# Keeping the transposed x in DRAM and moving 1/rms behind the input projections

## The chip, the cores and the metric

The kernel runs on one core of a Trainium2 chip. The metric is the time of one launch in microseconds on the device; the times before are a median of three runs. Engines are named as in the profile: PE (TensorE matmuls), PEld (its weight loads), DVE (VectorE), ACT (ScalarE), POOL (GpSimd) and SP (the engine whose queue issues most transfers).

## The reference

One layer of a decoder on 1024 prompt tokens and 64 sample tokens (8 sequences of 8), with D = 1024:

```
h     = x * rsqrt(mean(x*x) + eps) * g_mix            # RMS norm, per token
proj  = h @ w_in                                      # 1024 -> 1024 (RWKV) + 768 (conv) + 1536 (attention)
RWKV:      xs = p + (prev_token(p) - p) * mu_shift, then the recurrence on r, k, v, decay, a, g
short conv: u = c * x ; y = sum_j conv_w[j] * u[t-2+j] ; out = b * y
attention:  q = rmsnorm(q), k = rmsnorm(k) per head of 64; stick-breaking weights over k, v
x = x + concat(outputs) @ w_out
x = x + relu(rmsnorm(x) @ w_up)^2 @ w_down
x = x + sigmoid(rmsnorm(x) @ w_ple_gate) * (p @ w_ple_proj)
```

All is float32. Outputs are the new x for prompt and sample, the new key and value rows, and the recurrent states.

## The kernel before, in words

Activations stand transposed in SBUF, features on the partitions and tokens along a row. Each float32 operand of a large matrix product is split into a rounded part (`hi`) and its remainder (`lo`), and each product takes three matmuls: hi with hi, hi with lo, lo with hi.

The stages, in program order:

- **Front (L181 to L202).** Nine tiles of 128 tokens (the last has 64). Each is loaded (`x_tile`, four buffers `xt`), squared and summed on ACT (L189), and 1/rms is taken (L190, L192). DVE multiplies x by 1/rms and by the gain, which stands in `gbc` on all partitions (L193). PE transposes the result in eight 128x128 blocks (L198), ACT rounds it into `hT[0]` (L200), and DVE writes the remainder to `hT[1]` (L201).
- **RWKV projections (`rw_tile`, L319).** Eight tiles of 128 columns, each in three token chunks (`CH`: 384, 384, 320). A chunk is 24 matmuls (`gemm_t`, L169 to L171) into one of three PSUM banks (`acc`). ACT then reads the bank twice: a copy to `raw` (L330) and a product with 1 - mu to `xs` (L333, scale `om`); DVE adds mu times the shifted row (L334). `om` comes from the parameter rows, which PE transposes at L218. The first two tiles (`dwa`, `dg`) use the weights `w_da`. The weight loader `W.load` takes one transfer into `wr` (two buffers), a rounding on ACT (L158) and a subtraction on POOL (L159).
- **Recurrence and attention projections (`project`, L786 on).** The recurrent chain alternates with 30 projections whose results have tokens on the partitions: two tiles of 128 tokens by 256 columns to a bank (two banks, `gemm_sb`). ACT copies the bank to `nat` (L802), and for q and k it also squares it (L805).
- **Convolution and first attention half (`convolution`, L975 on, and `attention`).** The two generators take turns. For c the bank is copied to `cc` by ACT (L987); for x DVE multiplies the bank by `cc` into `ue` (L1002); for b DVE multiplies the bank by the convolved result `y` (L1027), which goes to `mix_s` in DRAM. In the attention, POOL sets masks (L920), DVE scans (L922), PE transposes the weights (L942).
- **MLP.** `Part` A holds tokens 0 to 511, `Part` B the other 576. `load_x` (L1292) reads x a second time from the input, in pieces of 128 tokens by 512 features (`xr`, four buffers shared with other temporaries), transposes each in four blocks on PE (L1302) and copies it to `self.x` on ACT (L1303). `load_mix` reads `mix_s` (L1287) and splits it; `out_proj` adds its products onto `self.x` (L1395). Part A's `load_x` stands at the end of the first attention half, part B's after the decoding attention.

The instructions of each engine run in a fixed order. A planner makes that order from the program and a model of durations: it issues what is ready by its own clock, in program order of priority, and takes the buffers as they become free. A wait on one instruction therefore holds everything behind it on the same engine or queue.

Of the kernel before, what the change touches and what calls it, by code (L numbers as in the profile page):

```python
# [48 lines left out]
def hybrid_step(ctx: ExitStack, tc: tile.TileContext, I, O):  # L49
# [6 lines left out]
    def f(t):  # L56
        return t.bitcast(F32)
# [38 lines left out]
    mix_s = dram.tile([8, 128, T], F32, name="mix_s")  # L96

# [8 lines left out]

    def x_tile(i):
        r = 128 if i < 8 else NS
        xt = xpool.tile([128, D], F32, name="xt", bufs=4)
# [4 lines left out]
    gbc = xpool.tile([128, D], F32, name="gbc")  # L114
    gm = I["g_mix"]
    SP.dma_start(gbc, bass.AP(tensor=gm.tensor, offset=gm.offset, ap=[[0, 128], [1, D]]))
# [59 lines left out]
    def w_cols(c0):  # L176
        return W.load(w_in[:, c0:c0 + 256])
# [3 lines left out]
    for i in range(9):  # L181
        if i == 1:
            w_da = w_cols(768)
        if i + 3 < 9:
            xts.append(x_tile(i + 3))
        xt, r = xts[i]
        st = xpool.tile([128, 2], F32, name="st", bufs=5)
        h = xpool.tile([128, D], F32, name="h", bufs=3)
        S.activation(h[:r], xt[:r], AF.Square, accum_out=st[:r, 0:1])  # L189
        S.activation(st[:r, 1:2], st[:r, 0:1], AF.Sqrt, bias=eps_rms[:r], scale=1.0 / D)  # L190
        rs = xpool.tile([128, 1], F32, name="rs", bufs=5)
        V.reciprocal(rs[:r], st[:r, 1:2])  # L192
        V.scalar_tensor_tensor(h[:r], xt[:r], rs[:r], gbc[:r], op0=ALU.mult, op1=ALU.mult)  # L193
        for g in range(2):
            pt = tr().rearrange("p (k t) -> p k t", k=4)
            for k in range(4):
                c = (4 * g + k) * 128
                PE.transpose(pt[:, k, :r], h[:r, c:c + 128], ident[:r, :r])  # L198
            dst = slice(i * 128, i * 128 + r)
            S.copy(hT[0][g][:, :, dst], pt[:, :, :r])  # L200
            V.tensor_sub(hT[1][g][:, :, dst], pt[:, :, :r], f(hT[0][g][:, :, dst]))  # L201
# [117 lines left out]
    def rw_tile(w, m, ct):  # L319

        raw = pe_tile("raw")
        xs = pe_tile("xs")
        G.memset(raw[:, 0:1], 0.0)
        rs3 = raw[:, E1:E1 + NB * 9].rearrange("p (b j) -> p b j", j=9)
        G.tensor_copy(rs3[:, :, 0], shT[:, ct, :])
        for t0, n in CH:
            ps = acc()
            gemm_t(ps, w, m, hT, t0, n)
            np_ = min(n, NP - t0)
            S.copy(raw[:, 1 + t0:1 + t0 + np_], ps[:, :np_])  # L330
            if np_ < n:
                S.copy(rs3[:, :, 1:9], ps[:, np_:n].rearrange("p (b j) -> p b j", j=NJ))
            S.activation(xs[:, t0:t0 + n], ps[:, :n], AF.Copy, scale=om[:, ct:ct + 1])  # L333
# [452 lines left out]
    def project(hf, n, w, i0):  # L786
# [15 lines left out]
        S.copy(flat, ps)  # L802
        if n < 2:
            sq = sbp.tile([128, 512], F32, name="sq", bufs=1)
            S.square(sq[:, :256 * ni], ps)  # L805
# [169 lines left out]
    def convolution():  # L975
# [3 lines left out]
        cc, ue, yu = [], [], []  # L979
        w = W.load(w_in[:, CV0 + 256:CV0 + 512])  # L980
        for j in range(2):
            t = cv.tile([128, LW], F32, name="cc", bufs=2)
            cc.append(t)
            for t0, n in CH:
                ps = gemm_cv()
                gemm_t(ps, w, j, hT, t0, n)
                S.copy(t[:, t0:t0 + n], ps[:, :n])  # L987
                yield
        w = W.load(w_in[:, CV0 + 512:CV0 + 768])
        for j in range(2):  # L990
            u = cv.tile([128, LW], F32, name="ue", bufs=2)
            ue.append(u)
# [28 lines left out]
        for j in range(2):  # L1021
            y = cc[j]
            for t0, n in CH:
# [239 lines left out]
    class Part:  # L1263
# [28 lines left out]
        def load_x(self, bank):  # L1292
            t0 = self.t0
            for i in self.tiles:
                r = 128 if i < 8 else NS
                for g in range(2):
                    xt = self.tmp("xr")
                    c = slice(g * 512, g * 512 + 512)
                    SP.dma_start(xt[:r], xp_in[i * 128:i * 128 + 128, c] if i < 8 else xs_in[:, c])
                    pt = bank().rearrange("p (k t) -> p k t", k=4)  # L1300
                    for k in range(4):
                        PE.transpose(pt[:, k, :r], xt[:r, k * 128:k * 128 + 128], ident[:r, :r])  # L1302
                    S.copy(self.x[:, 4 * g:4 * g + 4, i * 128 - t0:i * 128 - t0 + r], pt[:, :, :r])  # L1303
# [181 lines left out]
    A.load_x(acc)  # L1485
# [21 lines left out]
    B.load_x(tr)  # L1507
# [117 lines left out]
```

## Time and profile before

| | us |
|---|---|
| median of 3 runs | 1701.94 |
| lowest, highest | 1698.44, 1704.59 |
| profiled execution: span from first to last instruction | 1705.2 |
| profiled execution: own time | none is listed beside the span |
| PE busy | 1642.1 |
| DVE busy | 1055.6 |
| ACT busy | 790.8 |
| POOL busy | 698.7 |
| mean granted TensorE clock | 0.989 |

Shares are averages over stages with different limits, so the stages have to be read apart. The front ends at about 40 us, the RWKV projections run to about 160, recurrence and attention projections to about 440, convolution and first attention half to about 585, then come the second half, the decoding attention, the MLP and the gate. In the lines shown further down, a row of the timeline gives the start and length in us, the engine, the line and the operands, and in brackets how long the engine had been idle and for whom. A row of a group gives the total busy time and the mean length in ns. A row of waits gives the total in us, the number of waits and the longest. PE's records of matmuls are pipelined: the distance between starts, not the length of one, is what a matmul costs.

### The profile page before, as it was taken

What the parts mean: (1) busy time and instruction counts of PE and PEld (TensorE: products, weight loads), DVE (VectorE), ACT (ScalarE), POOL (GpSimd) and SP (SyncE); (2) the same over time, 40 slices, a digit from 0 to 9 for tenths busy, and PEclk for the clock granted to TensorE, in tenths of its full rate; (3) what the DMA queues carried; (4) which work ended last, traced back from release to release, by engine and by line L of the source; (5) the groups of instructions that cost most, each with busy time, mean ns of one, the idle gap of its engine ahead of it and who ended that gap; (6) DMA issues with size and microseconds to landing.
All of it is one profiled execution on the core that took longest, in us unless ns stands there. A gap on an engine that the chain in (4) does not pass through costs nothing.

```text
span 1705.2 us, 30695 instructions
## 1 busy us (share of the span) xinstructions
PE 1642.1 (96%) x11901; PEld 1481.8 (87%) x11901; DVE 1055.6 (62%) x1830; ACT 790.8 (46%) x1563; POOL 698.7 (41%) x754
## 2 busy tenths in 40 slices
PE   6999899999899898999999999999999999999998
PEld 5899888889888777888886777988999999999898
DVE  6266844555277749888853435277777777767432
ACT  6633433343354657666643344464543434437421
POOL 4123121123232565443334563356755455538210
PEclk9999999999999999999999999999999999999999
DMA  5144466325513764344235565422322322222211
GB/s 189 37 132 115 142 166 184 73 79 147 167 56 101 222 181 125 117 130 126 78 103 158 173 187 172 130 84 78 100 88 86 94 92 87 88 84 90 72 45 41
DMA packets 207060, 197.03 MB, mean 116 GB/s; under 512 B 58113, under 2 KB 172449, under 8 KB 206786
## 3 DMA queue, kind: packets, MB, share of 16 engines
q1 hardware_dynamic: 197186, 174.08, 34.4%
q0 software_dynamic: 5120, 16.78, 3.3%
q10 hardware_dynamic: 4608, 4.20, 1.0%
q8 instruction: 94, 1.54, 0.4%
q14 instruction: 52, 0.43, 0.1%
HBM read 158.03 MB, written 36.98 MB: 114 GB/s over the span
## 4 chain that ended last, share of the span: by engine, by line
PE 77%; DVE 9%; DMA 5%; ACT 3%; issue 3%; POOL 2%; SPq 2%; ACTq 0%; DVEq 0%; POOLq 0%
PE b L1093 13%; PE b L1095 13%; PE b L1094 12%; PE b L1440 3%; PE b L1442 3%; PE b L1441 3%; PE b L169 3%; PE b L170 3%; PE b L171 3%; PE b L797 2%; PE b L795 2%; PE b L796 2%; PE b L942 2%; DMA wr<-in_w_in 1%; DVE keep L922 1%
## 5 line engine op out<-in xcount | busy, mean ns | idle before, releaser
L1074 POOL TENSOR_TENSOR wl<-wr,wh 128x512 fp32r<-128x512 f32 x172 | 241.2, 1412 | 266.5 <-ACT wh L1073 227.7
L1073 ACT CAST wh<-wr 128x512 fp32r<-128x512 f32 x292 | 178.3, 621 | 300.6 <-PE b L1094 194.3
L1093 PE MATMUL b<-ah,wh 128*128 128x288 f32 (+1 forms) x768 | 253.6, 331 | 4.8 <-DVE x L1480 3.8
L1480 DVE TENSOR_TENSOR x<-b,x 128x288 f32<-128x288 f32 (+1 forms) x384 | 198.8, 528 | 90.9 <-PE b L1095 88.2
L1095 PE MATMUL b<-ah,wl 128*128 128x288 f32 (+1 forms) x768 | 252.3, 329 | 0.0
L1094 PE MATMUL b<-al,wh 128*128 128x288 f32 (+1 forms) x768 | 251.9, 328 | 0.0
L1093 PE MATMUL b<-nh,wh 128*128 128x512 f32 (+1 forms) x448 | 165.8, 370 | 3.1 <-DVE x L1480 1.4
L1094 PE MATMUL b<-nl,wh 128*128 128x512 f32 (+1 forms) x448 | 165.1, 369 | 0.0
L1095 PE MATMUL b<-nh,wl 128*128 128x512 f32 (+1 forms) x448 | 164.6, 368 | 0.0
L1093 PEld LDWEIGHTS b<-ah,wh 128*128 128x128 f32 x768 | 144.4, 188 | 17.3 <-DVE x L1480 6.6
L1095 PEld LDWEIGHTS b<-ah,wl 128*128 128x128 f32 x768 | 144.4, 188 | 10.1
L1094 PEld LDWEIGHTS b<-al,wh 128*128 128x128 f32 x768 | 144.5, 188 | 9.5 <-DVE al L1408 0.3
L795 PE MATMUL b<-wh,h_hi 128*128 128x256 f32 x432 | 127.6, 295 | 5.3 <-ACT sq L805 5.3
L797 PE MATMUL b<-wh,h_lo 128*128 128x256 f32 x432 | 126.9, 294 | 0.0
L796 PE MATMUL b<-wl,h_hi 128*128 128x256 f32 x432 | 124.8, 289 | 0.0
L169 PE MATMUL b<-h_hi,wh 128*128 128x384 f32 (+1 forms) x336 | 115.4, 344 | 1.9 <-ACT xs L333 1.3
L159 POOL TENSOR_TENSOR wl<-wr,wh 128x1024 fp32r<-128x1024 f32 x26 | 64.8, 2508 | 124.1 <-ACT wh L158 124.1
L1074 DVE TENSOR_TENSOR wl<-wr,wh 128x512 fp32r<-128x512 f32 x120 | 97.8, 817 | 28.1 <-ACT wh L1073 27.2
L170 PE MATMUL b<-h_lo,wh 128*128 128x384 f32 (+1 forms) x336 | 114.3, 340 | 0.3 <-DVE h_lo L201 0.3
L171 PE MATMUL b<-h_hi,wl 128*128 128x384 f32 (+1 forms) x336 | 113.2, 337 | 0.0
L922 DVE TENSOR_TENSOR_SCAN keep<-keep,onesq 128x128 f32<-128x128 f32 (+3 forms) x64 | 95.6, 1494 | 21.4 <-POOL keep L920 20.9
L1093 PEld LDWEIGHTS b<-nh,wh 128*128 128x128 f32 x448 | 84.3, 188 | 18.6 <-DVE x L1480 2.5
(427 smaller groups left out, 4284.6 us busy)
## 6 DMA issues: line engine op xcount, KB each, us to landing
wr<-in_w_up SPq DMA_DIRECT2D x64, 512.0 KB
wr<-in_w_down SPq DMA_DIRECT2D x64, 512.0 KB
wr<-in_w_in SPq DMA_DIRECT2D x26, 512.0 KB
wr<-in_w_out SPq DMA_DIRECT2D x16, 512.0 KB
xt<-in_x_prompt SPq DMA_DIRECT2D x8, 512.0 KB
stk_s<-sth ACTq DMA_DIRECT2D x32, 128.0 KB
stk_s<-stl SPq DMA_DIRECT2D x32, 128.0 KB
v_s<-spl SPq DMA_DIRECT2D x16, 256.0 KB
```

The lines of the kernel that those rows point to most:

```text
L169: PE.matmul(ps[:, :n], wh[:, k, c], a, start=(k == 0), stop=False)
L170: PE.matmul(ps[:, :n], wh[:, k, c], b, start=False, stop=False)
L171: PE.matmul(ps[:, :n], wl[:, k, c], a, start=False, stop=(k == nk - 1))
L795: PE.matmul(o, a, w[0][:, k, :], start=(k == 0), stop=False)
L796: PE.matmul(o, a, w[1][:, k, :], start=False, stop=False)
L797: last = PE.matmul(o, b, w[0][:, k, :], start=False, stop=(k == 7))
L1073: S.copy(h3, src)
L1074: (sub or G).tensor_sub(l3, src, f(h3))
L1093: PE.matmul(ps[:, :n], w(0, k, m), a, start=(k == 0), stop=False)
L1094: PE.matmul(ps[:, :n], w(0, k, m), b, start=False, stop=False)
L1095: PE.matmul(ps[:, :n], w(1, k, m), a, start=False, stop=(k == nk - 1))
L1480: V.tensor_add(p.x[:, m, t0:t0 + n], ps[:, :n], p.x[:, m, t0:t0 + n])
```

## The change

Three things are done together.

1. **x is transposed once, raw.** In the front, PE transposes x as loaded. DVE and ACT evacuate one half each into `xT` (256 tokens, two buffers). Per block of 128 features, ACT makes `hi` = x times g (the gain is now a column `gmT`, a scale of the activation), DVE makes `lo`. `xT` is stored to a new DRAM tensor `x_s` by ACT's queue. The squares come after that, in place, and leave 1/rms in the columns of `rsc`. `xt` has three buffers in place of four, the 512 KB load of `gbc` becomes one of 4 KB.
2. **1/rms goes to the results.** Nine small matmuls spread `rsc` over the partitions as `rbc` (128 x 1088), which is also stored to DRAM (`rb_s`). `rw_tile`: DVE multiplies the bank by `rbc` into `raw`; ACT makes `xs` from `raw`. `project`: the copy and the square become one ACT operation for each 128 tokens, with the column of `rsc` as scale. `convolution`: c is multiplied by `rb` (read back from `rb_s`) on DVE and once more on POOL, so that c times x has both factors; the result of b is multiplied by `rb` on POOL.
3. **The residual is read from `x_s`.** `load_x` becomes four transfers for each part, without transposes and copies.

```
-    for i in range(9):
-        if i == 1:
-            w_da = w_cols(768)
...
-        S.activation(h[:r], xt[:r], AF.Square, accum_out=st[:r, 0:1])
-        S.activation(st[:r, 1:2], st[:r, 0:1], AF.Sqrt, bias=eps_rms[:r], scale=1.0 / D)
-        V.reciprocal(rs[:r], st[:r, 1:2])
-        V.scalar_tensor_tensor(h[:r], xt[:r], rs[:r], gbc[:r], op0=ALU.mult, op1=ALU.mult)
...
-            S.copy(hT[0][g][:, :, dst], pt[:, :, :r])
-            V.tensor_sub(hT[1][g][:, :, dst], pt[:, :, :r], f(hT[0][g][:, :, dst]))
+    def x_sums(i):
+        xt, r = xts[i]
+        st = xpool.tile([128, 2], F32, name="st", bufs=5)
+        S.activation(xt[:r], xt[:r], AF.Square, accum_out=st[:r, 0:1])
+        S.activation(st[:r, 1:2], st[:r, 0:1], AF.Sqrt, bias=eps_rms[:r], scale=1.0 / D)
+        V.reciprocal(rsc[:r, i:i + 1], st[:r, 1:2])
+    for i0 in range(0, 9, 2):
+        ids = range(i0, min(9, i0 + 2))
+        t0, n = 128 * i0, min(256, T - 128 * i0)
+        if i0 == 2:
+            w_da = w_cols(768)
+        xT = xpool.tile([128, 8, 256], F32, name="xT", bufs=2)
+        for i in ids:
+            if i + 3 < 9:
+                xts.append(x_tile(i + 3))
+            xt, r = xts[i]
+            for g in range(2):
+                pt = tr().rearrange("p (k t) -> p k t", k=4)
+                for k in range(4):
+                    c = (4 * g + k) * 128
+                    PE.transpose(pt[:, k, :r], xt[:r, c:c + 128], ident[:r, :r])
+                dst = xT[:, 4 * g:4 * g + 4, 128 * (i - i0):128 * (i - i0) + r]
+                if g:
+                    S.copy(dst, pt[:, :, :r])
+                else:
+                    V.tensor_copy(dst, pt[:, :, :r])
+        for k in range(8):
+            hi, lo = (h[k // 4][:, k % 4, t0:t0 + n] for h in hT)
+            S.activation(hi, xT[:, k, :n], AF.Copy, scale=gmT[:, k:k + 1])
+            V.scalar_tensor_tensor(lo, xT[:, k, :n], gmT[:, k:k + 1], f(hi), op0=ALU.mult, op1=ALU.subtract)
+        S.dma_start(x_s[:, :, t0:t0 + n].rearrange("k p t -> p k t"), xT[:, :, :n])
+        for i in ids:
+            x_sums(i)
+    for t0, n in CH:
+        pt = tr()
+        for t in range(t0, t0 + n, 128):
+            r = min(128, T - t)
+            PE.matmul(pt[:, t - t0:t - t0 + r], rsc[:r, t // 128:t // 128 + 1].to_broadcast([r, 128]), ident[:r, :r],
+                      start=True, stop=True)
+        S.copy(rbc[:, t0:t0 + n], pt[:, :n])
+    S.dma_start(rb_s, rbc)
...
@@ rw_tile
-            S.copy(raw[:, 1 + t0:1 + t0 + np_], ps[:, :np_])
+            V.tensor_mul(raw[:, 1 + t0:1 + t0 + np_], ps[:, :np_], rbc[:, t0:t0 + np_])
+            S.activation(xs[:, t0:t0 + np_], raw[:, 1 + t0:1 + t0 + np_], AF.Copy, scale=om[:, ct:ct + 1])
...
-            S.activation(xs[:, t0:t0 + n], ps[:, :n], AF.Copy, scale=om[:, ct:ct + 1])
@@ project
-        S.copy(flat, ps)
+        for i, sc in enumerate(scales):
+            S.activation(nat[:, i], ps[:, 256 * i:256 * i + 256], AF.Copy, scale=sc)
...
-            S.square(sq[:, :256 * ni], ps)
+            for i, sc in enumerate(scales):
+                S.activation(sq[:, 256 * i:256 * i + 256], ps[:, 256 * i:256 * i + 256], AF.Square, scale=sc)
@@ convolution
+        rb = cv.tile([128, T], F32, name="rb")
+        SP.dma_start(rb, rb_s)
...
-                S.copy(t[:, t0:t0 + n], ps[:, :n])
+                V.tensor_mul(t[:, t0:t0 + n], ps[:, :n], rb[:, t0:t0 + n])
+                G.tensor_mul(t[:, t0:t0 + n], t[:, t0:t0 + n], rb[:, t0:t0 + n])
...
                 V.tensor_mul(y[:, t0:t0 + np_], ps[:, :np_], y[:, t0:t0 + np_])
+                G.tensor_mul(y[:, t0:t0 + np_], y[:, t0:t0 + np_], rb[:, t0:t0 + np_])
...
@@ Part
-        def load_x(self, bank):
...
+        def load_x(self):
+            for m in range(0, 8, 2):
+                SP.dma_start(self.x[:, m:m + 2], x_s[m:m + 2, :, self.t0:self.t0 + self.n].rearrange("k p t -> p k t"))
```

More of the change, by code (lines that the diff above doesn't have):

```diff
@@ L96, in hybrid_step @@
     mix_s = dram.tile([8, 128, T], F32, name="mix_s")
+    x_s = dram.tile([8, 128, T], F32, name="x_s")
+    rb_s = dram.tile([128, T], F32, name="rb_s")
     xp_in = I["x_prompt"][0]
@@ L113, in hybrid_step @@
     xts = [x_tile(0)]
-    gbc = xpool.tile([128, D], F32, name="gbc")
+    grow = xpool.tile([8, 128], F32, name="grow")
     gm = I["g_mix"]
-    SP.dma_start(gbc, bass.AP(tensor=gm.tensor, offset=gm.offset, ap=[[0, 128], [1, D]]))
+    SP.dma_start(grow, bass.AP(tensor=gm.tensor, offset=gm.offset, ap=[[128, 8], [1, 128]]))
     xts += [x_tile(i) for i in range(1, 3)]
@@ L180, in hybrid_step @@
     S.activation(pcs[:, 0, 0:1], eps_rms, AF.Sqrt)
-    for i in range(9):
-        if i == 1:
-            w_da = w_cols(768)
-        if i + 3 < 9:
-            xts.append(x_tile(i + 3))
+    rsc = consts.tile([128, 10], F32)
+    rbc = rp.tile([128, T], F32, name="rb_all")
+    gmT = xpool.tile([128, 8], F32, name="gmT")
+    pt = tr()
+    PE.transpose(pt[:, :8], grow, ident[:8, :8])
+    S.copy(gmT, pt[:, :8])
+    def x_sums(i):
         xt, r = xts[i]
         st = xpool.tile([128, 2], F32, name="st", bufs=5)
-        h = xpool.tile([128, D], F32, name="h", bufs=3)
-        S.activation(h[:r], xt[:r], AF.Square, accum_out=st[:r, 0:1])
+        S.activation(xt[:r], xt[:r], AF.Square, accum_out=st[:r, 0:1])
@@ L190, in hybrid_step @@
         S.activation(st[:r, 1:2], st[:r, 0:1], AF.Sqrt, bias=eps_rms[:r], scale=1.0 / D)
-        rs = xpool.tile([128, 1], F32, name="rs", bufs=5)
-        V.reciprocal(rs[:r], st[:r, 1:2])
[L193 to L201, printed above, removed]
+        V.reciprocal(rsc[:r, i:i + 1], st[:r, 1:2])
@@ L202, in hybrid_step @@
+    for t0, n in CH:
+        pt = tr()
+        for t in range(t0, t0 + n, 128):
[4 more added lines that the diff above has]
+    S.dma_start(rb_s, rbc)
+    S.copy(rsc[64:128, 9:10], rsc[0:64, 8:9])
+    S.copy(rsc[0:64, 9:10], rsc[64:128, 7:8])
     xpool.release()
@@ L978, in convolution @@
         CV0 = 1024
-        cc, ue, yu = [], [], []
+        cc, ue = ([cv.tile([128, LW], F32, name=n_, bufs=2) for j in range(2)] for n_ in ("cc", "ue"))
+        rb = cv.tile([128, T], F32, name="rb")
+        SP.dma_start(rb, rb_s)
         w = W.load(w_in[:, CV0 + 256:CV0 + 512])
         for j in range(2):
-            t = cv.tile([128, LW], F32, name="cc", bufs=2)
-            cc.append(t)
+            t = cc[j]
             for t0, n in CH:
@@ L990, in convolution @@
         for j in range(2):
-            u = cv.tile([128, LW], F32, name="ue", bufs=2)
-            ue.append(u)
+            u = ue[j]
             us3 = u[:, NP + 2:LW].rearrange("p (b j) -> p b j", j=NJ + 2)
@@ L1031, in convolution @@
                                  y[:, NP + 2:NP + 2 + NB * 10].rearrange("p (b j) -> p b j", j=10)[:, :, 0:NJ])
+                    G.tensor_mul(ue[j][:, 0:NS], ue[j][:, 0:NS], rb[:, NP:T])
                 yield
@@ L1290, in load_mix @@
                 V.tensor_sub(lo, t, f(hi))
-        def load_x(self, bank):
[L1293 to L1303, printed above, removed]
+        def load_x(self):
+            for m in range(0, 8, 2):
+                SP.dma_start(self.x[:, m:m + 2], x_s[m:m + 2, :, self.t0:self.t0 + self.n].rearrange("k p t -> p k t"))
         def norm(self, gain, bank, wide=False, pool=False):
@@ L1484, in hybrid_step @@
     A = Part(xpa, wka, hpa, 0, 512, ((0, 512),))
-    A.load_x(acc)
+    A.load_x()
     A.load_mix(range(0, 4))
@@ L1506, in hybrid_step @@
     B.load_mix(range(8))
-    B.load_x(tr)
+    B.load_x()
     out_proj(A, 4, 4)
```

9 lines of the change are left out of this document (7 added, 2 removed).

## The prediction

> **What bounds the kernel now.** I read the head and first part of the page, then the windows by stage.
>
> ```profile
> span 1705.2 us, 30695 instructions
> PE 1642.1 (96%) x11901; PEld 1481.8 (87%) x11901; DVE 1055.6 (62%) x1830; ACT 790.8 (46%) x1563; POOL 698.7 (41%) x754
> ...
> 0.00:40.00 40.00, 24.77 (x130) 21.81 (x130) 26.30 (x39) 26.34 (x54) 20.01 (x47) 0.96 0.64 202
> 40.00:100.00 60.00, 59.16 (x333) 54.08 (x334) 20.08 (x32) 34.16 (x59) 9.81 (x12) 0.97 0.11 37
> 100.00:160.00 60.00, 59.60 (x488) 58.07 (x487) 42.17 (x51) 26.09 (x44) 21.95 (x18) 1.00 0.44 140
> 160.00:440.00 280.00, 270.48 (x2880) 248.40 (x2879) 155.89 (x356) 98.53 (x204) 59.75 (x59) 0.98 0.52 136
> 440.00:555.00 115.00, 109.86 (x837) 97.49 (x838) 67.84 (x125) 50.55 (x110) 35.81 (x78) 0.97 0.33 95
> 555.00:605.00 50.00, 43.51 (x266) 36.72 (x264) 32.66 (x87) 30.22 (x68) 31.73 (x45) 0.97 0.70 216
> 1060.00:1085.00 25.00, 24.54 (x178) 22.87 (x177) 12.07 (x16) 14.25 (x25) 8.05 (x6) 1.00 0.66 217
> ```
>
> Columns of the windows: busy time of PE, PEld, DVE, ACT, POOL, then granted clock, DMA share, GB/s. TensorE is the bound nearly everywhere. The largest single loss is the front: 40 - 24.8 = 15.2 us idle, a quarter of the 63.1 us that PE is idle in the whole span (1705.2 - 1642.1). So the change is worth what it takes off PE where PE is full (1060 to 1085), plus what it does to the order in the front; where PE already waits (555 to 605), less.
>
> **Part 1, the second reading of x.** load_x (L1292) goes for both parts: 72 transposes, 18 ACT copies, 18 loads. Four plain loads per part replace them.
>
> ```profile
> 1064.16 0.60 PE L1302 MATMUL b<-ident,xr 128*128 128x128 f32 x4
> 1064.52 0.38 PE L1093 MATMUL b<-mh,wh 128*128 128x288 f32 x1
> 1075.52 2.32 PE L1302 MATMUL b<-ident,xr 128*128 128x128 f32 x16 [0.42 <-DMA xr<-in_x_prompt]
> 1077.77 0.40 PE L1093 MATMUL b<-mh,wh 128*128 128x288 f32 x1
> 1081.16 0.46 PE L1302 MATMUL b<-ident,xr 64*128 64x64 f32 x4
> PE b L1302 <- DMA xr<-in_x_prompt: 4.0, 2, 3.0
> 576.58 0.73 PE L1093 MATMUL b<-mh,wh 128*128 128x512 f32 x1
> 575.03 5.42 POOL L1074 TENSOR_TENSOR wl<-wr,wh 128x512 fp32r<-128x512 f32 x3 [0.92 <-ACT wh L1073]
> ```
>
> Part B (1060 to 1085): a group of four costs PE 0.36 us (1064.16 to 1064.52). Five such groups make 1.8; the run of 16 takes 2.25 (1075.52 to 1077.77) after a wait of 0.42; the last four some 0.4. Together 4.8 us. PE is busy 24.54 of 25 us there, so all of it comes off the end; the loads stay hidden if the DMA, busy 0.66 of its time, still brings w_out in time. If that cover fails, the bound is 0.
>
> Part A (555 to 605): 32 transposes at 0.09 are 2.9 us, and PE also waits 4.0 us for xr, 6.9 at most. But PE is already idle 6.5 us in this window, and the first out_proj matmul at 576.58 follows the weight split that starts on POOL at 575.03, which no transpose delays. So most of it turns into another wait. I take 2, bounds 0 and 6.9. The x loads (4 times 512 KB) still stand on SP's queue ahead of the mix loads, about as many bytes as today's.
>
> **Part 2, the front.** Today a tile goes: square, sqrt, reciprocal, times gain, transpose, round (ACT), remainder (DVE).
>
> ```profile
> 19.24 0.67 PE L169 MATMUL b<-h_hi,wh 128*128 128x384 f32 x1
> 24.07 0.34 PE L171 MATMUL b<-h_hi,wl 128*128 128x384 f32 x1
> 30.26 0.44 PE L169 MATMUL b<-h_hi,wh 128*128 128x384 f32 x1 [0.63 <-ACT h_hi L200]
> 36.93 1.73 PE L198 MATMUL b<-ident,h 128*128 128x128 f32 x16
> 38.84 0.85 DVE L221 TENSOR_SCALAR om<-par 128x8 f32<-128x8 f32 x1
> 39.73 1.05 ACT L333 ACTIVATE xs<-b,om 128x384 f32<-128x384 f32 x2 [0.48 <-DVE h_lo L201]
> 40.37 0.45 PE L169 MATMUL b<-h_hi,wh 128*128 128x384 f32 x1 [0.39 <-ACT xs L333]
> L189 ACT ACTIVATE h<-xt x9: 1051/1059/1082, 4.7 to 30.6; 128x1024 f32<-128x1024 f32 x8, 64x1024 f32<-64x1024 f32 x1
> L200 ACT CAST h_hi<-b x18: 392/584/618, 9.2 to 38.8; 128x512 fp32r<-128x512 f32 x16, 128x256 fp32r<-128x256 f32 x2
> L1316 ACT ACTIVATE nh<-x,par 128x512 fp32r<-128x512 f32 x8 | 5.5, 731 | 0.0
> L1453 ACT ACTIVATE c<-c 128x288 f32<-128x288 f32 x64 | 27.9, 442 | 24.2 <-DVE c L1452 24.2
> L852 ACTq DMA_DIRECT2D stk_s<-sth x32: 582/620/877, 188.2 to 414.0; - x32
> ```
>
> A 24-matmul chunk takes 4.2 us at full rate (19.24 to 24.07 with a cold start is 4.8); 16 transposes take 1.73. Until 40.37 PE has done 72 transposes (7.8 us) and two chunks (8.4): 24 us of 40 are lost, idle or at half rate. One cause is in the last three timeline rows: the bank of the first chunk is read twice, by the copy (L330) and by xs (L333), which needs om; om comes only at 39, so the dg tile, next on that bank, starts at 40.37. In the new kernel one DVE product frees the bank; xs reads raw from SBUF.
>
> New cost on ACT for two tiles: eight roundings of 128x256, estimated at 0.45 each (0.442 for 128x288, 0.731 for 128x512), 3.6; two evacuations 1.2; two squares with their small operations 2.8; one store issue 0.6. That is 8.2 against some 5.2 today. Four pairs, a last tile of about 4, and 4 for weight casts: 41 us from 4.7 on, so ACT ends at 46 if never idle. The squares also release xt, now three slots: tile 4 can load only after the square of tile 1, and so on.
>
> But squares can fill ACT's gaps, and PE is no longer held to two chunks. Laying the operations out by these durations: first GEMM at about 18, dg's first chunk at 25 (after the 1/rms of tiles 0 to 2), second chunks from 28 to 38, last chunk at 37 to 44. By 44 PE would have done five full chunks (20.8), one of 320 columns (3.5) and the transposes: 32 us, 12 lost, so 12 better. That is one end. The other: strict program order with ACT at 46, 46 - 16 = 30 lost, 6 worse. I take 5 better, nearer the middle than the layout, because the order is fixed beforehand and loads that come late hold a whole queue. The nine broadcasts (nearest row, a 0.11 us transpose) and the gain's transpose fall into idle time: 0; without it 1 to 2. The 4.45 MB store of x_s on ACT's queue shares the DMA engines (0.64 busy now, near nothing from 40 to 100): its cost is in the bounds.
>
> **Part 3, scaling the results.** The eight RWKV tiles: 24 copies leave ACT, 24 products of about 0.55 go to DVE (13 us).
>
> ```profile
> L447 DVE TENSOR_TENSOR xs<-b,xs x6: 482/548/558, 122.8 to 174.2; 128x384 f32<-128x384 f32 x4, 128x320 f32<-128x320 f32 x2
> PE b L795 <- ACT sq L805: 5.3, 1, 5.3
> ACT sq L805 <- DVE xs L447: 11.6, 1, 11.6
> L802 ACT COPY nat<-b 128x512 f32<-128x512 f32 x24 | 14.0, 585 | 53.2 <-PE b L797 51.7 <-issue 1.4
> L802 ACT COPY nat<-b 128x256 f32<-128x256 f32 x6 | 2.2, 372 | 12.0 <-PE b L797 11.0 <-ACT ss L808 1.0
> DVE AB L515 <- PE b L512: 18.4, 1, 18.4
> L1454 POOL TENSOR_TENSOR al<-c,ah 128x288 fp32r<-128x288 f32 x64 | 57.0, 902 | 25.6 <-ACT ah L1454 25.6
> POOL beta L920 <- ACT beta L915: 39.4, 19, 8.4
> PE b L942 <- DVE beta L924: 3.5, 1, 3.5
> ```
>
> Three banks of 4.2 us each cover the longer read-out (DVE product, then ACT, then DVE). Without cover the pattern is the one in rows two and three: DVE late, ACT waits in order 11.6, PE stands 5.3. I take 1, bounds 0 and 5. In the projections two 256-wide passes cost ACT 0.74 against 0.585, about 0.16 more, 24 times for nat and 16 times for sq: 6.4 us, behind two banks of 5 us. ACT also moves the recurrent chain there, so 1, bounds 0 and 4. In the convolution cc moves to DVE, whose queue stands up to 18.4 us at L515; rb must land before the first product. Twelve POOL products of about 1.1 (0.902 for 288 columns) and two small ones, 13.5 us, stand between the masks (L920) of the attention; POOL waits 39.4 us for ACT there, which covers most. Behind a late mask wait DVE's scan and then PE, as in the last row. The last product also delays the mix store by 1.1, with SP's queue behind it. I take 2, bounds 0 and 6. A gain here is excluded: nothing leaves PE.
>
> A row and a rule at this place: one front product took 3.16 us, others 1.28, while POOL worked beside it.
>
> ```profile
> 14.34 3.16 DVE L193 SCALAR_TENSOR_TENSOR h<-xt,rs,gbc 128x1024 f32<-128x1024 f32 x1
> 14.06 5.67 POOL L159 TENSOR_TENSOR wl<-wr,wh 128x1024 fp32r<-128x1024 f32 x2 [4.27 <-ACT wh L158]
> ```
>
> If every one of the fourteen POOL products held DVE for its length, 13.5 us would be added on DVE between 440 and 555, beyond my bound of 6. The Trainium skill, page "SBUF — State Buffer", section "Who interferes with whom", states it: GpSimd and a VectorE operation with two SBUF inputs exclude each other for a whole instruction. By that rule, the trace agrees in this one row.
>
> **The sum**, on the profiled execution: -4.8 (B) -2 (A) -5 (front) +1 (RWKV) +1 (projections) +2 (convolution) = -7.8, so a span of 1697.4. That execution's span lies 3.3 us above the median of the three runs, 1701.94 (nothing else around it is listed). I forecast 1701.94 - 7.8 = 1694 for the median.
>
> **Rivals.** (a) No change: the front's gain is eaten by ACT, part A's by other waits. Then -4.8 (B) + 4 (part 3) = -1, 1701. For it: ACT's 41 us in a front of 40. Against it: the bank held until 40.37. (b) Slower through one mechanism: ACT becomes the front's bound. The loads wait for squares behind eight roundings, and PE keeps program order: +6, with part B and A still won (-6.8) and the full bound of part 3's costs that also sit on ACT and DVE (+9): about +8, 1710. It decides once the last group's roundings end after about 49 (44 of the layout plus the 5 taken). (c) POOL's products hold the attention's scans: +13.5 in place of +2, so +4, 1706. (d) The transposes of both parts only covered waits, so that removing them frees nothing: -7.8 + 6.8, again 1701.
>
> **Chances.** Forecast 0.5; (a) and (d) together 0.28; (b) 0.15; (c) 0.07. A change under 0.3% (5 us) can't be told from none by this measurement. The forecast's own range is 1683 to 1699; its upper end is within 0.3%, and the better end of the front is 7 us beyond its middle. The range that leaves out 2 in 10 reaches 1681 to 1709. Faster 0.51, same 0.29, slower 0.2.
>
> **What would show it.** Right: L1302's line gone, out_proj of part B without gaps; PE's idle time in 0:40 under 12 us; dg's matmuls before 35 us; 440 to 555 no more than 2 us longer. Wrong: ACT over 36 us busy in 0:40 with PE waiting for the roundings; xt loads issued later than 30 us; PE waiting for mixl or wr in place of xr; longer waits of L922 for L920. A reordering of the planner far from the edits would make all of it wrong, in either direction.

## The result and the profile after

The change made the kernel slower: 1709.16 us (median of 11 runs, 1705.03 to 1710.62) beside 1702.35 for the kernel before in the same session, a ratio of 1.0043 (95% interval 1.0028 to 1.0057), +6.8 us. A second timing on another chip gave 1.0066 (1.0045 to 1.0087). The forecast was 1694, so it was wrong in sign; the time is near rival (b)'s 1710.

The profiled execution of the changed kernel lists 1709.11 beside its span of 1707.4. If the kernel before also lies 1.7 us above its span, its profiled execution took 1706.9, more than each of its 11 timed runs there (1695.94 to 1706.36). So differences between the two traces understate the loss; sizes of a whole kernel are taken from the timings.

The head of the page and the windows of the changed kernel, in the prediction's stages and columns:

```profile
span 1707.4 us, 30670 instructions
PE 1641.2 (96%) x11848; PEld 1476.5 (86%) x11848; DVE 1067.6 (63%) x1890; ACT 793.8 (46%) x1592; POOL 708.4 (41%) x768
...
0.00:40.00 40.00, 23.51 (x125) 20.27 (x125) 17.84 (x38) 31.39 (x69) 16.42 (x45) 1.00 0.84 273
40.00:100.00 60.00, 57.97 (x328) 52.15 (x328) 26.85 (x59) 32.94 (x63) 6.44 (x8) 0.97 0.19 65
160.00:440.00 280.00, 269.94 (x2928) 247.42 (x2923) 153.16 (x349) 110.92 (x248) 63.89 (x58) 0.98 0.51 135
440.00:555.00 115.00, 109.01 (x791) 96.14 (x791) 67.85 (x131) 44.63 (x98) 45.01 (x84) 0.96 0.35 100
555.00:605.00 50.00, 43.29 (x257) 35.90 (x256) 38.83 (x96) 26.05 (x61) 26.59 (x49) 0.80 0.67 211
1060.00:1085.00 25.00, 22.15 (x138) 19.66 (x137) 13.18 (x18) 10.74 (x17) 9.13 (x7) 1.00 0.74 252
```

53 matmuls have left PE (11901 to 11848 instructions), but its busy time has hardly moved (1642.1 to 1641.2). In the front PE now has 16.5 idle us of 40 instead of 15.2. ACT's share of the first 40 us rose from 26.3 to 31.4, and split in two it shows where. The windows of the changed kernel, and the waits of its first 60 us:

```profile
0.00:20.00 20.00, 7.37 (x32) 6.28 (x33) 4.00 (x9) 11.99 (x24) 11.90 (x41) 1.00 0.75 245
20.00:40.00 20.00, 16.14 (x95) 13.99 (x93) 13.83 (x30) 19.40 (x45) 4.51 (x5) 1.00 0.93 300
```

```profile
PE b L213 <- DMA xt<-in_x_prompt: 15.2, 5, 7.3
```

```profile
SPq L114 <- ACT st L196: 5.1, 2, 3.1
```

ACT is busy 19.40 of 20 us between 20 and 40, but only 11.99 of the first 20. PE's transposes stand 15.2 us for tiles of x, 4.6 of them for the first tile; the last row, of SP's queue, shows loads of x (L114) that stand for ACT. The timeline says more, and what the first bank waits for:

```profile
7.43 1.06 ACT L195 ACTIVATE xt<-xt 128x1024 f32<-128x1024 f32 x1
11.90 0.23 SPq L247 DMA_DIRECT2D prow<-in_gn_b  x1
12.26 0.36 SPq L114 DMA_DIRECT2D xt<-in_x_prompt  x1
18.63 3.96 PE L213 MATMUL b<-ident,xt 128*128 128x128 f32 x16 [7.26 <-DMA xt<-in_x_prompt]
22.25 0.53 PE L173 MATMUL b<-h_hi,wh 128*128 128x384 f32 x1
27.77 0.33 SPq L114 DMA_DIRECT2D xt<-in_x_prompt  x1
32.02 1.11 SPq L114 DMA_DIRECT2D xt<-in_x_sample  x1
38.91 0.46 ACT L232 COPY rb_all<-b 128x384 f32<-128x384 f32 x1
40.61 0.43 DVE L218 COPY xT<-b 128x256 f32<-128x256 f32 x1 [3.22 <-PE b L213]
42.85 0.54 DVE L364 TENSOR_TENSOR raw<-b,rb_all 128x384 f32<-128x384 f32 x1
43.45 0.69 PE L173 MATMUL b<-h_hi,wh 128*128 128x384 f32 x1
50.06 0.41 PE L173 MATMUL b<-h_hi,wh 128*128 128x320 f32 x1
```

PE's longest wait for x, 7.26 us until 18.63, is for the fourth tile. Its load (12.26) does not wait for a square: the first tile's square (L195) runs at 7.43, ahead of all roundings. The load stands in SP's queue behind the small loads of the parameter rows (`prow`, the last at 11.90), which waited 6.1 us for earlier transfers; in the kernel before, with four buffers, this load stands ahead of those rows and goes out before 3.4. Three later loads (23.73, 27.77 and 32.02) do wait for squares, 6.3 us in all, each issued as a square ends. The first matmul of the projections (the GEMM below) comes at 22.25 (before: 19.24). The first bank, held for `om` before, is now held for the broadcast 1/rms until 39.37, and then by the fixed order of DVE, which stands 3.22 us for the last tile of x and has other work ahead of the product: product at 42.85, next group at 43.45 instead of 40.37. The last chunk starts at 50.06.

To see where time goes from there I use an **offset**: for each ACT and DVE instruction that both traces have, its start in the changed kernel less its start in the kernel before, and the median of these over a stretch. All are worked out against the one profiled execution of the kernel before. The last column gives the time of the profiled execution, and behind it the median of that kernel's runs.

| kernel | 100 to 130 | 130 to 160 | 540 to 560 | 650 to 700 | 880 to 930 | 1030 to 1060 | 1090 to 1200 | end | profiled, median |
|---|---|---|---|---|---|---|---|---|---|
| the changed kernel | 5.6 | 4.4 | 9.3 | 8.0 | 8.4 | 2.7 | 1.8 | 2.0 | 1709.11, 1709.16 |
| the same, other chip | 4.1 | 2.9 | 8.4 | 7.2 | 7.7 | 8.6 | 7.2 | 6.9 | 1713.97, 1717.39 |
| x_slots | 4.5 | 3.4 | 5.8 | 9.4 | 9.8 | 10.9 | 9.3 | 9.9 | 1716.99, 1710.13 |
| front_dve | 3.5 | 2.5 | 0.0 | 5.3 | 5.6 | 1.6 | 0.3 | 1.1 | 1708.24, 1703.26 |
| mixl_first | 4.4 | 3.2 | 6.8 | 6.6 | 7.1 | 1.7 | -3.6 | -3.3 | 1703.84, 1704.94 |
| before_nudged | -0.1 | -0.1 | 3.7 | 1.1 | 6.9 | 7.5 | 6.5 | 6.6 | 1713.46, 1712.08 |
| before_nudged_2 | -3.5 | -3.5 | -8.8 | -9.3 | -5.4 | -5.8 | -5.4 | -5.4 | 1701.46, 1705.48 |

The 5.7 us that the changed kernel wins between 880 and 1030 are absent in its second profile (7.7 to 8.6): one execution's variation, not the change.

Two things limit what an offset can say. The profiled execution can lie far from the median: that of x_slots is the slowest of its 12. And the front's offset holds PE's granted clock. PE's program in before_nudged_2 is that of the kernel before up to 150 us, and yet it runs 3.5 us earlier at 100. The windows of the kernel before (first row) and of before_nudged_2:

```profile
30.00:40.00 10.00, 9.11 (x50) 8.01 (x50) 7.15 (x15) 5.43 (x14) 1.17 (x3) 0.83 0.19 55
```

```profile
30.00:40.00 10.00, 9.00 (x59) 7.90 (x60) 8.53 (x18) 5.88 (x14) 2.26 (x5) 1.00 0.20 55
```

The next 10 us have 0.83 and 1.00 too, with PE busy 9.63 in the kernel before. An estimate: 0.17 of 9.11 + 9.63 us is 3.2 of the 3.5 us. Against before_nudged_2, the front of the changed kernel is 6.4 to 9.1 us late instead of 2.9 to 5.6; it has 0.83 in a stretch of 10 us itself (40 to 50).

In the second half of the MLP, where I had expected 4.8 us, the gain is 0.9 (2.7 to 1.8). The timeline of the changed kernel shows the queue and the wait:

```profile
1059.95 3.01 SPq L1337 DMA_DIRECT2D x<-x_s  x4
1063.73 0.33 SPq L1330 DMA_DIRECT2D mixl<-mix_s  x1
1066.09 3.36 SPq L1330 DMA_DIRECT2D mixl<-mix_s  x3
1072.24 0.67 ACT L1332 CAST mh<-mixl 128x576 fp32r<-128x576 f32 x1 [5.55 <-DMA mixl<-mix_s]
1072.96 0.66 PE L1136 MATMUL b<-mh,wh 128*128 128x288 f32 x3 [1.34 <-ACT mh L1332]
```

Four loads of 576 KB go out ahead of the last four mix loads; ACT then stands 5.55 us for a mix piece, and PE for ACT.

### The profile page after: what moved, and what is told of

The parts are those of the page before. It is cut to its first block, busy times and chain, and to the rows that moved or that the text cites. A ratio compares the mean times of both kernels' runs of the same rounds, so it can differ in the third digit from the quotient of the medians.

```text
span 1707.4 us, 30670 instructions
## 1 busy us (share of the span) xinstructions
PE 1641.2 (96%) x11848; PEld 1476.5 (86%) x11848; DVE 1067.6 (63%) x1890; ACT 793.8 (46%) x1592; POOL 708.4 (41%) x768
```

## The experiments

All times are medians; each ratio is to the kernel before, timed in the same session.

| run | us | before | ratio, 95% interval |
|---|---|---|---|
| changed_again | 1717.39 | 1705.41 | 1.0066, 1.0045 to 1.0087 |
| x_slots | 1710.13 | 1705.41 | 1.0024, 1.0008 to 1.0041 |
| residual_old_no_store | 1713.35 | 1705.41 | 1.0042, 1.0026 to 1.0057 |
| projections_unscaled | 1712.43 | 1705.41 | 1.0043, 1.0030 to 1.0056 |
| front_dve | 1703.26 | 1701.42 | 1.0006, 0.9993 to 1.0019 |
| mixl_first | 1704.94 | 1701.42 | 1.0019, 1.0005 to 1.0033 |
| projections_dve | 1715.06 | 1701.42 | 1.0067, 1.0045 to 1.0090 |
| all_relieved | 1707.25 | 1701.42 | 1.0033, 1.0020 to 1.0045 |
| front_and_mixl | 1704.45 | 1705.23 | 0.9996, 0.9987 to 1.0005 |
| projections_fold | 1713.59 | 1705.23 | 1.0051, 1.0037 to 1.0064 |
| projections_fold_alone | 1716.00 | 1705.23 | 1.0066, 1.0047 to 1.0085 |
| evacuation_unscaled | 1711.56 | 1705.23 | 1.0037, 1.0024 to 1.0049 |
| changed_front_order | 1717.32 | 1706.48 | 1.0063, 1.0050 to 1.0076 |
| front_dve_changed_order | 1713.49 | 1706.48 | 1.0046, 1.0033 to 1.0060 |
| changed_nudged | 1716.60 | 1706.48 | 1.0063, 1.0044 to 1.0083 |
| before_nudged | 1712.08 | 1706.48 | 1.0035, 1.0022 to 1.0048 |
| before_nudged_2 | 1705.48 | 1704.13 | 1.0017, 1.0005 to 1.0028 |
| front_and_mixl_nudged | 1702.76 | 1704.13 | 0.9997, 0.9985 to 1.0009 |

### The front: the slots, or ScalarE?

The changed kernel once more, and one with room for all tiles of x:

> The changed kernel itself once more, beside the others on one chip. Theory S (stages): the loss sits in the kernel's order, so it repeats: 6 to 8 us over the kernel before, and the stretch up to 100 us is again 5 us late. Rival N (noise of one profile): the stage where the time is lost moves between executions, and the difference is under 4 us.

It came out about 12 us over the kernel before, more than either case, with an offset of 2.9 to 4.1 in the front.

```
-        xt = xpool.tile([128, D], F32, name="xt", bufs=XT)
+        xt = rp.tile([128, LW], F32, name="xt", tag="pe", bufs=12)[:, :D]
```

> Only one thing differs from the changed kernel: the nine loaded x tiles stand in the twelve large buffers that the RWKV stage uses later, so no load of x waits for a square to release its buffer. Theory S1 (the front is late because tile 3 is asked for at 12.3 us instead of 2.9, and each later one waits for a square): PE's idle time for x in 0 to 40 us falls from 15.2 to under 6, and the kernel is 4 to 7 us faster than the changed one, so within 3 us of the kernel before. Rival S2 (ACT is the bound of the front, 41 us of work): the loads come early, PE waits for ACT's roundings instead, and it gains under 2 us. Rival S3 (the 4.45 MB store of x_s fills the DMA engines): the loads come early but slow, gain 2 to 3 us.

The windows of x_slots, and PE's waits in its first 60 us:

```profile
20.00:30.00 10.00, 6.25 (x21) 5.25 (x21) 8.20 (x15) 9.87 (x24) 4.89 (x2) 0.50 0.84 268
30.00:40.00 10.00, 9.75 (x64) 8.93 (x62) 6.15 (x15) 10.00 (x23) 4.26 (x3) 0.98 0.70 226
```

```profile
PE b L213 <- DMA xt<-in_x_prompt: 5.8, 2, 4.6
PE b L173 <- ACT wh L162: 2.2, 1, 2.2
PE b L213 <- ACT h_hi L221: 1.9, 1, 1.9
```

PE's wait for x falls from 15.2 to 5.8 us, but waits for ACT's operations take its place, ACT is busy 19.87 of 20 us, and the GEMM still starts at 22.65. The offset at 100 to 160 is 3.4 to 4.5, as in changed_again (2.9 to 4.1). So more slots alone do not bring the front back, and ACT is full behind them. That ACT alone holds it there is not shown: PE's granted clock also fell, to 0.50 between 23 and 30, where the changed kernel has 1.00. Half of the 5.50 us that PE was busy there is 2.8 us (an estimate), most of the 3.5 us by which its idle time up to 60 us fell (18.5 to 15.0). By timing theory S1 fits better: the whole ran 7 us faster than changed_again. The trace cannot show where, since its execution (1716.99) was slower than that of changed_again (1713.97).

Next came the store of x_s and the second reading of x as it was before:

> The changed kernel without its part 1: x is not stored to x_s, and the residual is read from the input and transposed as before. The front and the scaling of results stay. Theory S: it loses the 3 us that the residual path gained after 555 us (offset 9.5 to 8.0 in part A, 2.9 to 1.6 in part B) and wins 1 to 2 us from a free DMA in the front: 1 to 2 us slower than the changed kernel. Rival S3 (the store is the front's cost): the front is 4 us faster, the whole 1 to 2 us faster than the changed kernel.

The DMA engines were freed (share 0.52 in place of 0.93 between 20 and 40), yet the offset at 100 to 160 stayed at 4.3 to 5.5. That speaks against the store as the front's cost, but does not settle it: here too PE's granted clock was 0.50 between 23 and 30, with PE busy 6.35 of 7 us. And by timing the run was 4.0 us faster than changed_again (1713.35 beside 1717.39), where theory S had it slower and S3 1 to 2 us faster. What the store and the loads from `x_s` cost together is open.

For the wait of the bank for 1/rms:

> The changed kernel with the results of the RWKV projections read from their bank as before, by two ScalarE copies, with 1/rms left out there; nothing of this evacuation waits for 1/rms. Theory B (the wait of the first bank for the broadcast 1/rms holds the GEMM behind it): the third group of columns starts at about 40 as before instead of 43.45, and the time is 3 us below the changed kernel. Rival S2 (the last columns' roundings on ScalarE hold the GEMM at 50 us in any order): the chunks of 320 still start near 50, the offset at 100 to 160 us stays within 1 of the changed kernel's 4.4 to 5.6, and the time within 1.5 us; two ScalarE reads in place of one may add up to 1.

The copy, which now waits for nothing but ACT's queue, came at 41.94, only 0.9 before the product that it replaces. The offset at 100 to 160 was 5.9, no better than the changed kernel's (in a profiled execution of 1723.28, the slowest of its runs; their median is 1711.56). The last chunk came earlier than S2 expected (45.65, not 50), without an earlier end of the stage. The bank's wait for 1/rms was real, but ACT would have kept it about as long.

Then ScalarE's load was taken off:

```
-            S.activation(hi, xT[:, k, :n], AF.Copy, scale=gmT[:, k:k + 1])
+            if k % 2:
+                V.tensor_scalar(hi, xT[:, k, :n], gmT[:, k:k + 1], None, op0=ALU.mult)
+            else:
+                S.activation(hi, xT[:, k, :n], AF.Copy, scale=gmT[:, k:k + 1])
...
-        S.copy(rbc[:, t0:t0 + n], pt[:, :n])
+        V.tensor_copy(rbc[:, t0:t0 + n], pt[:, :n])
```

> Three edits to the changed kernel's front, nothing else: x has the twelve ring slots of x_slots (its loads wait for no square), the roundings of odd k go to VectorE (20 of 40, about 9.3 us of ScalarE work at the 466 ns of x_slots' row), and the evacuation of the broadcast 1/rms goes to VectorE as well. Theory S2 (ScalarE bounds the front: 19.4 of 20 us busy between 20 and 40): ScalarE falls to about 14 of 20 there, the broadcast 1/rms is ready about 6 us earlier (37 instead of 43.4), and the offset to the kernel before at 100 to 160 us falls from about 4.5 to between -2 and +1; the whole gains about 4 on x_slots, to about 1706 where x_slots had 1710. Rival S3 (TensorE's own order is the bound: the transposes of x, now without 1/rms, and the GEMM chunks behind the broadcast): ScalarE has free time and the offset stays at 4 to 5, the time at about 1710. Rival S4 (VectorE takes ScalarE's place: 20 roundings more on 13.8 to 19 us of 20): VectorE over 19 of 20 and the offset stays or grows, 1710 to 1713.

The window of front_dve and PE's waits in its first 60 us:

```profile
20.00:40.00 20.00, 15.59 (x82) 13.70 (x82) 17.89 (x35) 17.39 (x38) 11.45 (x5) 0.74 0.87 280
```

```profile
PE b L213 <- DMA xt<-in_x_prompt: 7.9, 3, 4.6
PE b L173 <- ACT h_hi L224: 2.7, 1, 2.7
PE b L213 <- ACT xT L216: 1.7, 1, 1.7
PE b L174 <- DVE h_lo L225: 1.7, 2, 1.5
PE b L173 <- DVE raw L366: 1.4, 1, 1.4
```

The time came out about as S2 gave (1.0006; its 1706 beside 1705.41 is 1.0003), the front itself not: the offset at 100 to 160 fell only to 2.5 to 3.5, ACT and DVE share the load at 17.4 and 17.9 of 20, and PE waits for x and for each of them in turn, with its clock at 0.74. Five further kernels below have this front, and their offset at 130 to 160 is 0.0 to 1.9; in eight profiles with the changed kernel's front it is 2.9 to 5.9. So the slots and the sharing together win some 3 us of the front, not all of it.

### The mix loads

```
-    B.load_x()
+    with tc.issue_after(B.last_mix.ins):
+        B.load_x()
```

> The changed kernel with one edit in order: the four loads of the transposed x for the second half of the MLP are issued behind the last load of the mix instead of ahead of it. Theory (the loads of x, 576 KB each, delay the last mix loads by about 5.5 us and with them the output projection, so that part B gave 1.3 of 4.8): the idle 5.55 us of ScalarE before the mix rounding go, the stretch 1060 to 1085 is 3 to 3.5 us shorter than in the changed kernel, the whole about 3 us shorter than changed_again. Rival (the projection is held by its weights or by the throttle): the same time as changed_again, within 1.5 us. Second rival: the x loads now land late and the residual adds wait: no gain, with waits of VectorE for x in the output projection.

The window of mixl_first, its waits between 1060 and 1085, and its queue:

```profile
1060.00:1085.00 25.00, 25.00 (x175) 24.10 (x174) 12.76 (x19) 11.27 (x19) 11.03 (x9) 1.00 0.77 262
```

```profile
ACT mh L1332 <- DMA mixl<-mix_s: 3.5, 4, 1.3
```

```profile
1062.58 4.12 SPq L1330 DMA_DIRECT2D mixl<-mix_s  x4
1066.75 1.96 SPq L1337 DMA_DIRECT2D x<-x_s  x4
```

PE is now full (25.00 of 25), ACT stands 3.5 us for mix pieces in place of 7.5, and the offset falls by 5.3 us there (1.7 to -3.6) instead of 0.9. By timing the ratio is 1.0019 against 1.0043 and 1.0066. This edit moves 42 rows of PE's program, all between 1000 and 1100 us, and nothing ahead of them, so it is the cleanest comparison of the study: the theory holds.

### The projections

> The changed kernel, with the attention projections evacuated as before: one copy and one square for 512 columns, no factor 1/rms (left out for q, k and v). Theory S: the stretch from 150 to 430 us, where the offset grows from 5.6 to 9, keeps its offset, and the kernel is 2 to 3 us faster than the changed one. Rival: the 6.4 us of extra ACT time are hidden and the growth comes from the planner's order: under 1 us.

> The changed kernel with 1/rms applied in the q, k, v projections by one VectorE product of 512 columns (the two token tiles' 1/rms broadcast) that also evacuates the bank, and one ScalarE square of the result, instead of two ScalarE copies and two squares that each read the bank. Theory (the doubled ScalarE passes, 54 of 470 ns and 36 of 476 ns between 160 and 440 in place of 27 and 18 of twice the width, cost the 5 us that projections_unscaled gained): the time is like projections_unscaled, about 5 us below changed_again. Rival (the bank's second reader was no cost; what projections_unscaled gained was the scaled copies' start-up on a busy ScalarE, and VectorE, 54 of 100 us busy, adds a wait of its own ahead of the sums of squares): between changed_again and 3 us below it; TensorE's wait for the normalised k and q, 6.2 us, stays or grows.

> The three edits together: front_dve, projections_dve and mixl_first on the changed kernel. If the causes are those named (ScalarE in the front 4 to 5 us, the doubled passes 5 us, the mix loads 3 us) and they add, the time is about 12 us below changed_again, so 3 to 5 us below the kernel before (about 1701 where that has 1705). If they overlap, because what one frees is lost at the next wait, it is 1705 to 1710.

Leaving 1/rms out gave about 5 us (1712.43 beside 1717.39), but not in the stretch that theory S named: the offset still grew, from 3.6 at 130 to 160 to 9.1 at 400 to 440. Moving it to DVE gave nothing (1.0067). The three edits together gave 1.0033, slower than both cases on record (1705 to 1710 where the kernel before has 1705.41 is at most 1.0027), and some 6 us slower than front_and_mixl, which lacks the move to DVE (0.9996). So I folded 1/rms into the head's norm:

```
-            S.activation(nat[:, i], ps[:, 256 * i:256 * i + 256], AF.Copy, scale=sc)
+            S.copy(flat, ps)                     # q and k; v as before
...
+            V.scalar_tensor_tensor(ss3, ss3, 1.0 / 64, e[:, :, None].to_broadcast([128, ni, 4]),
+                                   op0=ALU.mult, op1=ALU.add)
-            S.activation(ss[:, :m], ss[:, :m], AF.Sqrt, bias=eps_rms, scale=1.0 / 64)
+            S.activation(ss[:, :m], ss[:, :m], AF.Sqrt)
```

> front_dve and mixl_first together on the changed kernel, without projections_dve, which cost 3 to 6 us in all_relieved. If the two gains add (front_dve 1.0006 and mixl_first 1.0019 beside 1.0043 to 1.0066 of the changed kernel: 0.4 to 0.6% and 0.25 to 0.45%), the ratio to the kernel before is 0.997 to 0.998, so about 4 us below it. If the front's gain is lost again before the second half of the MLP, 1.0000 to 1.0015.

> front_and_mixl, and q and k evacuated as before by one ScalarE copy and squared by one: their 1/rms goes into the small term under the root of the head's norm instead (one VectorE operation on 128 by 8 per group), and only v, 9 groups of 27, is scaled by two copies. Theory (the doubled ScalarE passes cost the 4 to 5 us that projections_unscaled gained): 3 to 4 us below front_and_mixl, a ratio of about 0.995. Rival (that gain was the variation from one execution's order of work to another's; ScalarE has half of this stretch free, 1.0 of each 2.7 us): within 1 us of front_and_mixl.

> The same edit of q and k alone on the changed kernel. Theory: 3 to 5 us below the changed kernel, a ratio to before of 1.002 to 1.003. Rival: 1.0043 to 1.0066, as the changed kernel.

The windows of front_and_mixl (first row) and of projections_fold:

```profile
160.00:440.00 280.00, 269.27 (x2893) 246.12 (x2892) 154.37 (x356) 108.74 (x244) 62.11 (x58) 0.98 0.51 133
```

```profile
160.00:440.00 280.00, 269.87 (x2865) 247.58 (x2866) 154.99 (x363) 99.22 (x214) 62.10 (x58) 0.96 0.51 131
```

The fold took 9.5 us off ACT, with DVE, POOL and PE's busy time as before, and the kernel was 9 us slower. Both theories on record fall. The rows show one more difference, the granted clock, 0.96 in place of 0.98; 0.02 of PE's 270 busy us would be 5.4 us (an estimate), but why it fell is not shown. On the changed kernel alone the fold gave 1.0066, as the rival had it. front_and_mixl's two gains did not add: 0.9996, between the two cases.

### The order

What else differs is the order. The planner lays out every engine anew after any edit. Of PE's rows 700 to 6200 (5500, about 100 to 1000 us), 946 stand in another order in the changed kernel than before, 2000 in front_dve against the changed kernel, and 1900 in projections_fold against front_and_mixl. Transposes of the identity into a spare bank change the order with next to no work, or bring one kernel to the order of another:

```
+    pt = tr()
+    PE.transpose(pt[:, :128], ident, ident)      # 1, 2, 3, 16 or 24 of them
```

> The changed kernel and 16 transposes of the identity into a spare bank at about 43 us, whose result nobody reads; with them the planner comes to front_dve's order of the matmuls behind the front (16 of 5500 moved against it, 1998 against the changed kernel). The 16 cost 1.7 to 4.5 us by the transposes' rows (107 ns of 4 passes of a ready row up to 273 ns). Theory O (the order behind the front makes most of the difference between the changed kernel and front_dve): a ratio of 1.001 to 1.003 in spite of them. Theory S2 (ScalarE in the front makes it): the changed kernel's 1.0043 to 1.0066 and the 16 transposes' price, 1.006 to 1.009.

> front_dve and 24 such transposes, by which the planner comes to the changed kernel's order behind the front (7 of 5500 rows moved apart from the 24). They cost 2.6 to 6.5 us. Theory O: the changed kernel's ratio, 1.005 and their price, 1.006 to 1.009. Theory S2: front_dve's 1.0006 and their price, 1.002 to 1.0045.

> The changed kernel and one such transpose, 0.3 us at most; 475 of the 5500 matmuls come in another order. Theory S2: like the changed kernel, 1.0043 to 1.0066. Theory O: anywhere between 0.999 and 1.009.

> The kernel before and two such transposes, 0.6 us at most; 2079 of the 5500 matmuls come in another order. If the order is worth little (S2), 1.0000 to 1.0010. Theory O: over 1.002 or under 0.998; over 1.004 would mean that the kernel before owes as much to its order as the change lost.

Two idle transposes cost the kernel before 5.6 us (1.0035). Its front is unmoved (offset -0.1); the loss comes between 160 and 560 (3.7) and between 650 and 930 (5.8). So the order alone weighs about as much as the change. But the changed kernel gave 1.0043 to 1.0066 in its own order and 1.0063 in two others. Its loss is thus not one unlucky order. changed_front_order, the changed kernel in front_dve's order, gave 1.0063, inside S2's range and far from theory O's 1.001 to 1.003: the order alone does not bring front_dve's gain. front_dve in the changed kernel's order gave 1.0046 with its 24 transposes, just above S2's 1.0045 and below O's 1.006. Their price is only an estimate (2.6 to 6.5 us), so this run does not exclude that the order has a share.

One more order of the kernel before, and of the best one:

> The kernel before and one transpose of the identity into a bank of the projections, 0.3 us; 723 of the 5500 matmuls behind the front come in another order. If the kernel before owes its time to one lucky order: over 1.002 again. If before_nudged hit a bad order: 0.999 to 1.001.

> front_and_mixl and three transposes of the identity, under 1 us; 769 of the 5500 matmuls come in another order. If its time is the work's and not the order's: 0.999 to 1.0015. If its 0.9996 hangs on the order: 1.002 to 1.006.

The kernel before: 1, 1.0035, 1.0017 in three orders; the last lies between the two cases on record. The changed kernel: about 1.0055 (mean of two timings), 1.0063, 1.0063 (the last with 16 transposes). The mended kernel: 0.9996, 0.9997 in two. By the medians none of the changed kernel's orders is as fast as the slowest order before (1.0043 and 1.0035, with intervals that overlap), and the mended one is at the fastest. So the loss is mostly the change's work and its own transfers, with the order worth up to 0.35% in these three, of which the kernel before has the fastest, and two edits, the roundings shared with DVE (with slots for all of x) and the mix loads first, bring it back to the time before, not below: both intervals hold 1. Beside the two other orders of the kernel before, the mended one is 0.2 to 0.4% faster.

## Why the prediction was wrong

**The front: -5 forecast, +3 to +5.5 found** (offset 2.9 to 5.6 at 100 to 160 in two profiles of the changed kernel). The step that failed is "squares can fill ACT's gaps", and with it the layout whose last chunk starts at 37 to 44. ACT's work was less than the sum's 41 us (busy 35.2 us between 4.7 and 45.3), but its gaps lay in the first 20 us, where x was missing. Between 20 and 40 it had none (19.40 of 20): the squares there stood among the roundings, and three loads of x waited for squares. The last rounding ended at 45.3, close to the 46 of my strict order, which the layout had set aside. The layout's first GEMM at 18 became 22.25, its last chunk 50.06. "One DVE product frees the bank" was wrong too: I had seen `om` hold the bank and did not ask what holds it next. It was the broadcast 1/rms and then DVE's own queue, and dg's chunk came at 43.45, not 25. Rival (b) had much of the mechanism: ACT full, loads that wait for squares, PE in its fixed order. But PE's longest wait was not for a square, and the time fits by luck. Its terms were +6 for the front (4.4 found), -6.8 for parts A and B (-2.2 found) and +9 for part 3 (4.9 found), and its point of decision, 49 for the last roundings, was not reached. Of my signs, the x loads after 30 us came (32.02), ACT over 36 us busy in the first 40 did not (31.4).

**Part B: -4.8 forecast, -0.9 found.** The size was right, -5.3 with the mix loads first. What failed is the cover I named, "the loads stay hidden if the DMA still brings w_out in time". It was not w_out that came late but mixl: "wrong" sign number three of my list.

**Part A: -2 forecast, -1.3 found** (9.3 to 8.0, and in the second profile 8.4 to 7.2). The number fits, but it is not shown to be the loads: between the same stretches the offset falls by 2.6 in before_nudged, which has the old loads, and grows by 5.3 in front_dve, which has the new ones.

**Part 3: +4 forecast, 4.9 found** between 130 to 160 and 540 to 560 (4.4 to 9.3; 5.5 in the second profile). The sum fits, the reason is not shown: before_nudged grows by 3.8 in the same stretch without any of this work, and the ways of easing the projections gave -5 (left out), 0 (on DVE), 0 and +9 (folded, in two kernels). The mask waits that I feared, POOL's L920 for ACT, 40.6 before between 440 and 605, did not grow, nor did DVE's for the masks (13.9 before, 10.0 after). The waits of the changed kernel between 440 and 605:

```profile
POOL beta L960 <- ACT beta L955: 34.3, 19, 10.3
POOL cc L1069 <- DVE cc L1068: 12.8, 5, 4.5
```

Summed for the profiled execution: +4.4 (front) +4.9 (part 3) -1.3 (part A) +0.4 (to 880) -5.7 (880 to 1030, this execution) -0.9 (part B) +0.2 = +2.0, the offset at the end; without the -5.7 it is 7.7, near the 6.8 timed. Against my sum of -7.8, the front is off by 9.4 and part B by 3.9; that is 13.3 of the 15 us of the miss. The sum is the account of one execution: in the stretches of parts 3 and A, before_nudged moves by about as much without the change. Rival (c), 13.5 us on DVE between 440 and 555, came true only in small. Of DVE's operations beside POOL's fourteen products, three with both inputs in SBUF took 0.5 to 0.6 us more than the shortest of their form (scans of 384 columns 1.53 and 1.56 against 0.95, a product of 512 columns 1.18 against 0.67), while the products that read a bank beside them kept their length (L552: 0.42 and 0.43).

**Still open:** what the scaling of the projections costs by itself, how the front's loss divides among ACT, the slots, PE's half rate and the store, why x_slots gained 7 us, and which pairs of rows make one order slower than another. An experiment that fixes the planner's order and removes only the work was not tried.

## What to carry to other kernels

When work moves from one engine to another, lay out the receiving engine's queue, with what each of its operations releases: a square that frees a load slot is part of the load's path. A transfer that replaces computation is paid for by what stands behind it on its queue. And where a planner orders the program, nudge the unchanged kernel first: here two idle transposes cost 5.6 us, so no single-edit difference below that is evidence by itself. Look, too, where the profiled execution lies among the timed ones before an offset is read from it.

## What the runs showed that I had not expected

PE's granted clock fell to half after quite short waits. The windows of x_slots, with some of PE's rows in and between them:

```profile
12.00:14.00 2.00, 2.00 (x14) 2.00 (x14) 1.38 (x4) 2.00 (x5) 0.00 (x0) 1.00 1.08 388
14.00:16.00 2.00, 0.37 (x4) 0.13 (x2) 0.99 (x4) 2.00 (x6) 0.00 (x0) 1.00 1.02 405
16.00:18.00 2.00, 1.50 (x8) 1.13 (x8) 0.83 (x3) 0.31 (x1) 0.00 (x0) 0.70 0.84 208
30.00:32.00 2.00, 2.00 (x13) 2.00 (x12) 1.46 (x1) 2.00 (x7) 1.83 (x2) 0.89 1.08 296
```

```profile
16.32 1.50 PE L213 MATMUL b<-ident,xt 128*128 128x128 f32 x8 [1.95 <-ACT h_hi L221]
25.64 0.52 PE L173 MATMUL b<-h_hi,wh 128*128 128x384 f32 x1
26.60 0.52 PE L173 MATMUL b<-h_hi,wh 128*128 128x384 f32 x1
30.86 0.34 PE L173 MATMUL b<-h_hi,wh 128*128 128x384 f32 x1
31.38 0.33 PE L173 MATMUL b<-h_hi,wh 128*128 128x384 f32 x1
```

PE worked through to 14.4, stood 1.95 us for ACT, and the clock halved between 16 and 18; it was full again only from 30 on, and three GEMM matmuls took 0.96 us in between and 0.52 after. (The 1.00 of 12 to 14 is no proof of full rate all along: the 32 transposes from 8.09 to 14.37 came 0.2 us apart, where 16 at 36.93 in the kernel before took 1.73, 0.11 each.) The Trainium skill, page "TensorE: Matmul & The Clock Gate", part 1 on the clock gate, states that the clock halves after an idle window of about 3.4 us and comes back after a busy one. The half rate agrees; the idle piece ahead of it is shorter here.

Over the whole kernel the mean granted clock was 0.986 to 0.994 in 26 runs of the kernel before and 0.978 to 0.986 in 17 of the changed one. Over the 26 runs, 0.001 less goes with 1.2 us more; over the 11 runs of the changed kernel's first session it goes with none. Whether the lower clock is a cause of the loss or a sign of PE's waits is not settled: between 555 and 605 it was 0.80 instead of 0.97, while PE's busy time stayed the same (43.29, before 43.51).
